# The opening of a fused mixer and feed-forward kernel: first transfers on one queue, in other cuts, and warming products in another order

## The chip, the cores and the metric

The kernel runs on one core of a Trainium2 chip. The metric is the device time of one execution in microseconds; the figure for a kernel is the median over its runs. A profile of one execution gives, for every instruction, its engine, start and length, and for every DMA its issue and landing.

## The reference

One layer of a transformer-like block, batch 1, 256 tokens, width 1024, all in float32. A vector `c` gives six modulation rows (two shifts, two scales, two gates); the block has a mixer and a convolutional feed-forward, each with a modulated input, a gated residual and a layer norm.

```python
mod = silu(c) @ w_ada + b_ada
sh1, sc1, g1, sh2, sc2, g2 = split(mod, 6)
h = x * (1 + sc1) + sh1
y = token_mixer(h, w_in, w_proj_moba, w_proj_ret, w_out)   # proj = h @ w_in, attention + retention
x = layer_norm(ALPHA * x + g1 * y, ln1_g, ln1_b)
h = x * (1 + sc2) + sh2
y = conv_ffn(h, w_ff_gate, w_ff_up, ff_conv_w, ff_conv_b, w_ff_down)
x = layer_norm(ALPHA * x + g2 * y, ln2_g, ln2_b)
```

The change lies wholly in the first microseconds: the first part of `silu(c) @ w_ada`, on which the first tile of `h`, and with it the first product of `h @ w_in`, depends.

## The kernel before

Every weight is streamed once from HBM. A float32 product is made from three: a weight tile `raw` is split by ScalarE into a rounded part `whi` (line 284) and by VectorE into the remainder `wlo` (line 287), the activations likewise into `hh` and `hl`, and TensorE adds `hh*whi`, `hh*wlo` and `hl*whi` (line 301 in the first stage). The order of all work is written out by hand; the queues are in order.

The first stage goes over the eight 128-row slices j of the contraction dimension. For slice j the unit `m{j}` holds the columns of `w_ada` (transposed) that give scale and shift of these 128 channels, 128 x 2048 numbers, 1 MB. VectorE multiplies it with the row `srow` of silu(c), the same in all partitions, and sums along the row; with `bcol` added these are scale and shift (`mod`). Then `h1` makes the tile `hh` from `xT` (line 267 for slice 0), and the tiles `a{j}`, `b{j}`, `g{j}` of `w_in` are split and multiplied.

The list `UNITS` is the order of the loads. `load_A` takes the next one; four buffers `raw` (`RAW_BUFS`) are filled at the start, later ones as buffers come free. `load_cuts` issues one DMA for each pair of column bounds: the first piece on queue `q0`, the others on SP's queue; `then` is called behind the first piece. For `a0b0` that is `load_x(0)`, the load of `xT` for slice 0 (`AYa` in the profile). For `m0`, `q0` is ACT's queue; all other loads go on SP's.

Before all units SP issues `first`, a table of 128 x 56 numbers: `c` in columns (`cT`) and biases. The opening is then:

- ScalarE loads its activation table (line 131), VectorE sets 512 columns of `srow` to zero (line 190), and TensorE multiplies these zeros with each other (line 192, widths `WARM`, results unused).
- With `first` there, line 196 and 197 make silu(c) in columns, and eight transposes (line 204, in `rows`) spread it into two PSUM banks as the row, 512 columns each.
- TensorE makes two products of columns of m0 that nobody reads (line 213, `BUSY`).
- `ada0` (lines 233 to 242) makes scale and shift of slice 0 by four reductions over 512 columns of m0 each (line 238), the first two with the first bank, and adds up (line 242). m0's columns lie in the order scale and shift of the first 512 channels, then of the other 512. ScalarE copies the banks to `srow` (line 206) for the later slices.
- Line 267 makes `hh` of slice 0 in two parts of 128 tokens, `halve("a0", 512)` splits `a0`, and line 301 begins.

Behind the first stage come further projections, attention and retention, the output projection, layer norm, feed-forward and the last norm, all fed by the same stream on SP's queue.

## Time and profile before

| | us |
|---|---|
| median of 3 runs | 423.86 |
| lowest, highest | 423.75, 424.02 |
| profiled execution, its own time | 423.81 |
| its span, first to last instruction | 422.1 |
| TensorE busy in the span | 412.2 |
| VectorE busy | 369.8 |
| ScalarE busy | 245.6 |

Rows of the profile read: line of the kernel, engine, operation, tile written <- tiles read, shape, then count, busy time and length. PE is TensorE, PEld its weight loads, DVE VectorE, ACT ScalarE, POOL GpSimd, SP the engine that issues most DMAs; a q behind a name is its queue. q1 is SP's DMA queue, q10 ACT's. Rows of the timeline begin with start and length, and in brackets stand idle time before and what ended it; consecutive instructions of one kind are merged (x4), with the length of the group. A product of two float32 operands shows as two passes. Matmul lengths are modelled ends; starts are the better measure.

### The profile page before, as it was taken

The page shows a single profiled execution, that of the slowest core. Times are in us where ns is not written, and L with a number is a line of the kernel's source. Part 1 is how long each engine was busy: PE and PEld are TensorE (multiplying, and loading weights), DVE is VectorE, ACT ScalarE, POOL GpSimd, SP SyncE. Part 2 cuts the span into 40 slices and gives each one's busy share as a digit, 9 for nine tenths or more (in the row PEclk, how much of TensorE's full clock was granted, in tenths as well). Part 3 has the DMA queues.
Part 4 walks back from the last instruction along what each step waited for, and adds up shares of the span by engine and source line. Part 5 has one row for each costly group of instructions (what it writes and reads, how often), then busy time and mean ns, then how long its engine had stood idle before and what let it go on. Part 6 is the DMA issues. An engine that isn't in the chain of part 4 may idle for free.

```text
span 422.1 us, 5794 instructions
## 1 busy us (share of the span) xinstructions
PE 412.2 (98%) x2104; PEld 347.9 (82%) x2104; DVE 369.8 (88%) x613; ACT 245.6 (58%) x397; POOL 14.0 (3%) x26
## 2 busy tenths in 40 slices
PE   7999999999999999999999999999999999999993
PEld 4888888888888888888888898888888888888883
DVE  5979899978999999899787887999999888789976
ACT  4666568687876387534554886555555445455700
POOL 0000000100000000001000001000000010012200
PEclk9999999999999999999999999999999999999998
DMA  8997997786479778788672094975865776550002
GB/s 309 405 410 304 419 415 286 242 319 226 186 264 352 280 254 332 313 301 327 233 283 99 2 346 183 374 293 194 302 267 214 278 285 231 187 187 2 1 25 75
DMA packets 18540, 105.58 MB, mean 250 GB/s; under 512 B 2256, under 2 KB 3536, under 8 KB 7760
## 3 DMA queue, kind: packets, MB, share of 16 engines
q1 hardware_dynamic: 16992, 99.70, 62.4%
q0 software_dynamic: 1376, 4.99, 3.2%
q10 hardware_dynamic: 144, 0.52, 0.4%
q8 instruction: 16, 0.26, 0.2%
q14 instruction: 12, 0.10, 0.1%
HBM read 104.15 MB, written 1.06 MB: 249 GB/s over the span
## 4 chain that ended last, share of the span: by engine, by line
PE 96%; DVE 2%; DMA 1%; issue 0%; DVEq 0%; ACT 0%
PE P L115 17%; PE P L116 17%; PE P L117 17%; PE P L124 16%; PE P L301 13%; PE P L126 8%; PE P L688 1%; PE P L691 1%; PE P L690 1%; PE P L993 1%; DMA first<-in_first 1%; PE P L1048 1%; PE P L1071 1%; PE P L1095 1%; DVE unread L238 1%; PE P L1156 0%
## 5 line engine op out<-in xcount | busy, mean ns | idle before, releaser
L1277 DVE TENSOR_TENSOR wlo<-raw,whi 128x1024 fp32r<-128x1024 f32 x118 | 141.7, 1219 | 13.5 <-ACT whi L1263 13.4
L1263 ACT ACTIVATE whi<-raw 128x1024 fp32r<-128x1024 f32 x118 | 122.1, 1056 | 40.8 <-DMA raw<-in_wpr 10.0
L115 PE MATMUL P<-whi,AH 128*128 128x512 f32 x160 | 63.3, 396 | 0.0
L117 PE MATMUL P<-whi,AH 128*128 128x512 f32 x160 | 62.3, 390 | 0.0
L116 PE MATMUL P<-wlo,AH 128*128 128x512 f32 x160 | 62.3, 389 | 0.0
L301 PE MATMUL P<-whi,AH 128*128 128x512 f32 x160 | 41.6, 390 | 0.8 <-DVE AH L267 0.8
L124 PE MATMUL P<-AYa,whi 128*128 128x512 f32 x144 | 39.2, 393 | 0.0
L227 DVE CUSTOM_DVE_ANT_0 junk<-raw,srow 128x1024 bf16<-128x1024 f32 x32 | 39.0, 1219 | 0.0
L124 PE MATMUL P<-AYb,whi 128*128 128x512 f32 x144 | 38.6, 390 | 0.0
L301 PEld LDWEIGHTS P<-whi,AH 128*128 128x128 f32 x160 | 30.0, 188 | 7.8 <-ACT whi L284 1.6
L115 PEld LDWEIGHTS P<-whi,AH 128*128 128x128 f32 x160 | 30.0, 188 | 6.6 <-issue 0.7
L117 PEld LDWEIGHTS P<-whi,AH 128*128 128x128 f32 x160 | 30.0, 188 | 6.4
L116 PEld LDWEIGHTS P<-wlo,AH 128*128 128x128 f32 x160 | 30.1, 188 | 5.9
L465 ACT ACTIVATE A<-P 128x256 f32<-128x256 f32 x36 | 13.7, 381 | 34.4 <-PE P L126 32.5
L124 PEld LDWEIGHTS P<-AYb,whi 128*128 128x128 f32 x144 | 27.0, 188 | 6.0
L284 ACT ACTIVATE whi<-raw 128x512 fp32r<-128x512 f32 (+1 forms) x26 | 20.6, 822 | 16.9 <-DMA raw<-in_strm 15.4
L287 DVE TENSOR_TENSOR wlo<-raw,whi 128x512 fp32r<-128x512 f32 (+1 forms) x26 | 23.3, 935 | 5.5 <-ACT whi L284 5.5
L124 PEld LDWEIGHTS P<-AYa,whi 128*128 128x128 f32 x144 | 25.1, 190 | 3.6
L126 PEld LDWEIGHTS P<-AYa,wlo 128*128 128x128 f32 x144 | 22.0, 189 | 2.8
L301 PE MATMUL P<-wlo,AH 128*128 128x512 f32 x80 | 23.2, 390 | 0.0
L126 PE MATMUL P<-AYb,wlo 128*128 128x256 f32 x144 | 23.1, 283 | 0.0
L126 PE MATMUL P<-AYa,wlo 128*128 128x256 f32 x144 | 22.9, 282 | 0.0
(302 smaller groups left out, 733.2 us busy)
## 6 DMA issues: line engine op xcount, KB each, us to landing
raw<-in_ada SPq DMA_DIRECT2D x16, 1024.0 KB, 5.0
raw<-in_wup SPq DMA_DIRECT2D x11, 1024.0 KB, 4.9
raw<-in_wgate SPq DMA_DIRECT2D x11, 1024.0 KB, 5.1
raw<-in_wdown SPq DMA_DIRECT2D x11, 1024.0 KB, 5.0
raw<-in_winB SPq DMA_DIRECT2D x10, 1024.0 KB, 7.7
raw<-in_strm SPq DMA_DIRECT2D x8, 1024.0 KB, 7.7
raw<-in_strm SPq DMA_DIRECT2D x13, 512.0 KB, 6.9
raw<-in_winGr SPq DMA_DIRECT2D x4, 1024.0 KB, 6.2
```

The source lines that it names most:

```text
L115: pe.matmul(o, lh, rh, start=start, stop=False)
L116: pe.matmul(o, lh, rl, start=False, stop=False)
L117: pe.matmul(o, ll, rh, start=False, stop=stop)
L124: pe.matmul(o, wh[:, k * 128:(k + 1) * 128], x2[k], start=k == 0, stop=False)
L126: pe.matmul(o[:, :256], wl[:, k * 128:(k + 1) * 128], x2[k][:, 0], start=False, stop=k == n - 1)
L227: dve.tensor_tensor_reduce(out=nobody(j if own else None), in0=raw, in1=srow, scale=1.0, scalar=0.0, op0=OP.mult, op1=OP.add, accum_out=mo ...
L284: act.activation(hi[:, o], raw[:, o], AF.Copy)
L287: dve.tensor_tensor(lo[:, o], raw[:, o], f(hi[:, o]), OP.subtract)
L301: pe.matmul(pa[b0 + c // 512 * 2 + t], x[xi][:, j, t * 128:(t + 1) * 128], ws[k][:, c:c + 512], start=first and (xi, k) == (0, 0), stop=la ...
L465: act.activation(t, p[:, 256:], AF.Copy)
L1263: act.activation(hi, src, AF.Copy)
L1277: dve.tensor_tensor(lo, src, f(hi), OP.subtract)
```

## The change

- m0's first piece is issued by SP instead of ACT, so behind `first` on the same queue, and m0 comes in three pieces of 512, 512 and 1024 columns instead of two of 1024.
- `a0b0` comes in two pieces of 1024 columns (a0, then b0) instead of four of 512; `xT` of slice 0 stays behind the first piece.
- The zeroed columns of `srow` are set in two steps, 128 and 384 columns, and the unused products are of 128 and 448 columns instead of 512 and 160. (The loop pairs three banks with two widths, so there are two products, as before.)

```diff
-WARM = (512, 160)
+WARM = (128, 448)
...
-        cuts = Q4 if u == "a0b0" else HALVES if j < 4 and u[0] in "mb" else (0, 2048)
+        cuts = (0, 512, 1024, 2048) if u == "m0" else (0, 1024, 2048) if u == "a0b0" else HALVES if j < 4 and u[0] in "mb" else (0, 2048)
...
-        load_cuts(t, src, cuts, (lambda: load_x(0)) if u == "a0b0" else None, act if u == "m0" else sp)
+        load_cuts(t, src, cuts, (lambda: load_x(0)) if u == "a0b0" else None, sp if u == "m0" else sp)
...
-    dve.memset(srow[:, :512], 0.0)
-    for b, w in zip((4, 5), WARM):
+    for c in (0, 128), (128, 512):
+        dve.memset(srow[:, c[0]:c[1]], 0.0)
+    for b, w in zip((4, 5, 4), WARM):
         pe.matmul(bank(b)[:, :w], srow[:, :128], srow[:, :w], start=True, stop=True)
```

## The prediction

> **What bounds the kernel now.** I read the page's first parts, then the chain that ended last, then the opening in order of time.

> ```profile
> span 422.1 us, 5794 instructions
> PE 412.2 (98%) x2104; PEld 347.9 (82%) x2104; DVE 369.8 (88%) x613; ACT 245.6 (58%) x397; POOL 14.0 (3%) x26
> PE 96%; DVE 2%; DMA 1%; issue 0%; DVEq 0%; ACT 0%
> 0.81 3.12 DMA first<-in_first
> 4.50 1.10 PE P L204 x4
> 5.62 0.40 DVE unread L238
> 6.93 0.60 DVE unread L238
> 8.39 0.36 DVE AH L267
> 8.88 54.72 PE P L301 x240
> 415.02 0.43 DVE A7b L578
> ```

> The last rows are pieces of the chain (start, length, what). From 8.88 to 415 us it is TensorE without a gap that matters; before it stands a serial opening: small table, four transposes, VectorE's reductions over m0, the first stationary tile. So the change can win what L301 starts sooner, if the feed afterwards keeps up. The profiled execution took 423.81 us (its span and 1.7 us around it), 0.05 below the 423.86 median; I subtract from the median.

> The opening in order of time (start, length, engine and line; x counts merged instructions):

> ```profile
> 0.80 0.40 ACTq L102 DMA_DIRECT2D raw<-in_strm  x1
> 0.81 0.37 SPq L136 DMA_DIRECT2D first<-in_first  x1
> 0.88 0.06 DVE L141 MEMSET epst<- 128x1 f32 x1 [0.88 <-PEq L1423]
> 1.01 0.48 DVE L190 MEMSET srow<- 128x512 f32 x1
> 1.23 0.89 SPq L102 DMA_DIRECT2D raw<-in_strm  x2
> 1.24 1.28 ACT L131 ACT_TABLE_LOAD   x1 [1.24 <-PEq L1423]
> 1.55 2.61 PE L192 MATMUL P<-srow 128*128 128x512 f32 x4 [1.55 <-DVE srow L190]
> 2.57 1.06 PE L192 MATMUL P<-srow 128*128 128x512 f32 x1
> 3.42 0.34 PEld L192 LDWEIGHTS P<-srow 128*128 128x128 f32 x1 [0.52 <-issue]
> 3.69 0.47 PE L192 MATMUL P<-srow 128*128 128x160 f32 x1
> 5.17 0.54 PE L204 MATMUL P<-ident,sc 128*128 128x128 f32 x2
> 5.54 0.49 PE L204 MATMUL P<-ident,sc 128*128 128x128 f32 x3
> 5.87 2.21 PE L213 MATMUL P<-raw 128*128 128x512 f32 x4
> 7.53 1.14 ACT L284 ACTIVATE whi<-raw 128x512 fp32r<-128x512 f32 x2
> 8.39 0.60 DVE L267 TENSOR_SCALAR AH<-AYa,mod 128x128 fp32r<-128x128 f32 x2
> ```

> **The change, step by step.** *Warming products.* The one-column memset takes 0.06, that of 512 columns 0.48, so about 0.06 plus 0.42/512 per column: 128 columns end at 1.01 + 0.165 = 1.18, and TensorE, which began 0.06 after the memset, begins at 1.24 instead of 1.55. The other 384 columns (0.38) end before the first product does. Each product is two passes; the second 512-column pass runs from 2.57 to 3.42, 1.66 ns a column, and the very first took 0.17 more. The loop pairs three banks with two widths, so two products remain, 128 + 448 = 576 columns: 576 x 2 x 1.66 ns = 1.91, and the engine is free at 1.24 + 0.17 + 1.91 = 3.32 us. Before it was free at 3.69 + 0.27 = 3.96 and then waited for the transposes' input until 4.50.

> *The small table.* It now has the DMA engines alone at first; before, the first half of m0 (512 KB) started on ACT's queue 0.01 us earlier. What that did, in packets (count, MB, share) by queue, q1 being SP's and q10 ACT's, for 1.8 to 1.9 us and for 3.4 to 3.5 us:

> ```profile
> q10 hardware_dynamic: 4, 0.02, 87.2%
> q1 hardware_dynamic: 41, 0.01, 41.1%
> q10 hardware_dynamic: 12, 0.05, 131.4%
> q1 hardware_dynamic: 1, 0.00, 0.6%
> ```

> 41 small packets went in the first tenth of a microsecond, and one was still going at 3.4 us, between 4 KB packets of m0. The table's landing at 3.93 (0.81 + 3.12) is 0.4 us behind its last packets. Alone, its packets should be through by about 2.2 and it lands near 2.6: that is my value; the other end is 3.93, no change. From landing to transposes it was 0.57 (3.93 to 4.50), so anything up to 2.75 is hidden under the warming products. ACT is no obstacle: without its DMA issue (0.40) its 1.28 us table load starts about 0.84 and the small activation behind it (0.20) ends near 2.35. So the transposes begin at 3.32, and the first reduction 1.12 later (4.50 to 5.62 before): 4.44, a gain of 1.18 at this point. It does not reach the end of the opening, as the loads show.

> *m0 and what is behind it.* SP issues as many DMAs up to g0 as before (first, three for m0, two for a0b0, x0, g0; before first, one, four, x0, g0), ACT's issue goes. m0's first piece is issued at 1.23 instead of 0.80.

> ```profile
> raw<-in_strm SPq DMA_DIRECT2D x1, 512.0 KB, 4.7
> raw<-in_strm SPq DMA_DIRECT2D x1, 256.0 KB, 5.0
> AYa<-in_strm SPq DMA_DIRECT2D x1, 128.0 KB, 4.9
> 2.17 0.43 SPq L163 DMA_DIRECT2D AYa<-in_strm  x1
> GB/s 0 41 224 353 418 369 399 389 416 414 410 400 407 406 414 410 410 389 406 418 393 422 386 405 410 438 438 385 410 426 377 408 432 410 373 74 16 106 319 426
> ```

> The last line is GB/s in each microsecond from 0 to 40: from 4 to 34 us the DMA engines are full, so landings go by bytes, not by issue. Second half of m0: issue 1.23, landing 5.93. Next quarter of a0b0: 1.70 + 5.0 = 6.70; x0: 2.17 + 4.9 = 7.07. Now x0 stands behind 1024 columns of a0 instead of 512: 512 KB (0.524 MB) at the 414 GB/s that large packets reach is 1.27, x0 itself 0.37 (6.70 to 7.07): 5.93 + 1.27 + 0.37 = 7.57, plus a delay d of the stream in front of it. One part is known: half of m0 now goes in 2 KB packets, which a0b0's rows from 5 to 8 us show at 386 GB/s (mean of 369, 399, 389): 0.09 more than at 414. The other is the later start: at most the 0.43 by which the issue moves; below, the stream no longer shares its first microsecond with small packets (224 GB/s from 2 to 3 us against 400 later), which from 2.25 on could put it 0.16 ahead. So d lies between -0.07 and 0.52; no row is nearer to one end, and I take the middle, 0.22: x0 at 7.79.

> [...]

> *VectorE's opening.* m0's cuts of 512 columns are wanted at 4.44 and 5.05 and land, counted back from 5.93 + d at 395 GB/s, at 4.16 and 4.82. The last is wanted 1.31 after the first reduction (5.62 to 6.93), at 5.75, and lands at 6.15: VectorE waits 0.4. From that third reduction to L267 it is 1.46 (6.93 to 8.39): 6.15 + 0.04 + 1.46 = 7.65. L267 also reads x0, which ends last: 7.79 + 0.04 = 7.83. L301 follows 0.49 later (8.88 - 8.39): **8.32 us, 0.56 sooner**. By the same count the table may land as late as 3.3 at no cost. ACT needs whi of a0: a0's half lands at 5.93 + 1.27 + 0.22 = 7.42, two activations end at 7.42 + 1.14 = 8.56, the first near 8.0, and the second is read by the third product, half a microsecond after the start: hidden, by 0.3.

> *Will the feed keep up?* TensorE moves 0.56 earlier; the stream, d later behind m0, gets back 0.18 when a0b0 goes in large packets, so it is 0.04 late. The tightest rows, tile a1 and, for comparison, tile b3's stationary part:

> ```profile
> 20.75 0.33 SPq L102 DMA_DIRECT2D raw<-in_a1a  x1
> 26.26 2.43 PE L301 MATMUL P<-whi,AH 128*128 128x512 f32 x10
> 26.45 0.60 ACT L269 ACTIVATE AH<-AYb,mod 128x256 fp32r<-128x256 f32 x1 [0.24 <-DVE mod L260]
> 30.60 1.06 ACT L284 ACTIVATE whi<-raw 128x1024 fp32r<-128x1024 f32 x1 [1.49 <-DMA raw<-in_a1a]
> 31.69 1.23 DVE L287 TENSOR_TENSOR wlo<-raw,whi 128x1024 fp32r<-128x1024 f32 x1 [1.85 <-ACT whi L284]
> 33.74 0.39 PE L301 MATMUL P<-wlo,AH 128*128 128x512 f32 x1
> ```

> a1's low part is ready at 31.69 + 1.23 = 32.92 and read at 33.74: 0.82 of slack, of which 0.56 + 0.04 is used. b3's stationary tile is ready at 27.05 and read eight products into the group of ten, 28.08: 1.03. So 0.22 is left and no stall comes; after 34 us the stream idles (74, 16 GB/s), loads wait for buffers and move with TensorE. Sum: 423.86 - 0.56 = **423.30 us**.

> **Rivals.** (A) *The stream is the new bound.* With d = 0.52, x0 lands at 8.09, L267 starts at 8.13 and gains 0.26: 423.60. For it: every load to 34 us is DMA-paced, ACT waits 1.49 for a1; against it: the shared first microsecond.
> (B) *The table lands as late alone as beside m0.* Then the transposes stay at 4.50 and nothing moves: 423.86. Against it stand the 41 packets in the first 0.1 us.
> (C) *Slower: TensorE's clock falls back.* L192 ran 0.85 us per 512-column pass, while the four passes of L213 took 2.21 with a stall in them, and L301 began 0.80 after they ended (5.87 + 2.21 = 8.08) at full pace. If the warm state is missed or lost before L301, as many microseconds as it took to warm up run at half pace (1.55 to about 5.4, where the transposes' starts close up: two from 5.17, 0.2 apart, then three within 0.22 from 5.54): 1.9 lost, 423.30 + 1.9 = 425.2. For it: 96 columns fewer are warmed with, and the gap grows. Transposes at 3.32, eight at 0.21 to 5.0, L213 2.21 to 7.2, so 1.1 of idleness before 8.32. Against it: work begins 0.31 sooner and has no hole (0.54 before, 3.96 to 4.50), so 3.85 us of it are over at 5.1, and 0.80 of idleness cost nothing. It decides if 1.1 does. [...]
> (D) *More than forecast.* The stream starts at full rate, d = -0.07 or less: x0 at 7.50, L267 at 7.54, VectorE's own chain (5.86 + 0.04 + 1.46 = 7.36) is no bound: gain 0.85 or more, 422.95.

> **How the numbers follow.** Chances: forecast 0.54, A 0.20, B 0.06, C 0.09, D 0.11. A measurement of this kernel tells about 0.2%, 0.85 us, from no change; forecast, A and B lie within it: 0.80; D beyond it, 0.11; C slower, 0.09. The forecast's own range is 423.1 to 423.5; with A, B and half of D, 422.9 to 424.0, which leaves out C and the other edge of D.

> **What would show it.** TensorE's first product at about 1.24; the table landing before 3.3 (2.6 expected); L204 at 3.32; first L238 at 4.44 and the third after a wait for m0's last cut, at 6.2; L267 at 7.83, waiting for x0 and not for `mod`; L301 at 8.32 with passes at full pace; no wait of TensorE at a1 near 33. Wrong if L204 still waits for the table, if L267 stands at 8.1 or later behind x0, if L301's first passes take 0.43 apart, or if a gap of TensorE between 17 and 34 us gives the start back.

## The result: slower by 4.9 us, and the profile after

| | before | after |
|---|---|---|
| median, us | 423.93 (4 runs) | 428.81 (4 runs) |
| lowest, highest | 423.75, 424.02 | 428.08, 429.12 |
| profiled execution | 423.81 | 429.12 |
| its span | 422.1 | 427.4 |

The ratio is 1.0114, 95% interval 1.0102 to 1.0126. The forecast was 423.30 with a range of 422.9 to 424.0: wrong in sign and far outside the range. When the changed kernel was run again later it gave 425.01 to 428.99 (median 427.83), while the kernel before stayed within 0.6 us beside it; single executions of the changed kernel therefore differ by more than most effects below.

The opening after, from the timeline, in order of time (start, length; the bracket gives idle time before and what ended it). Lines from 190 on are one higher than before.

```profile
1.15 2.29 PE L193 MATMUL P<-srow 128*128 128x128 f32 x4 [1.15 <-DVE srow L191]
2.48 0.21 ACT L197 ACTIVATE sc<-first 128x8 f32<-128x8 f32 x1 [0.18 <-DMA first<-in_first]
3.24 1.92 PE L205 MATMUL P<-ident,sc 128*128 128x128 f32 x8
4.39 0.69 DVE L239 CUSTOM_DVE_ANT_0 unread<-P,raw 128x512 bf16<-128x512 f32 x1 [1.22 <-PE P L205]
4.94 3.10 PE L214 MATMUL P<-raw 128*128 128x512 f32 x4
5.53 0.69 DVE L239 CUSTOM_DVE_ANT_0 unread<-P,raw 128x512 bf16<-128x512 f32 x1 [0.44 <-DMA raw<-in_strm]
9.43 0.69 DVE L239 CUSTOM_DVE_ANT_0 unread<-P,raw 128x512 bf16<-128x512 f32 x1 [3.20 <-DMA raw<-in_strm]
10.62 1.15 ACT L285 ACTIVATE whi<-raw 128x512 fp32r<-128x512 f32 x2 [3.69 <-DMA raw<-in_strm]
11.04 0.60 DVE L268 TENSOR_SCALAR AH<-AYa,mod 128x128 fp32r<-128x128 f32 x2
11.54 2.04 PE L302 MATMUL P<-whi,AH 128*128 128x512 f32 x4 [3.49 <-DVE AH L268]
```

Down to the first reduction (4.39) everything came within 0.15 us of the forecast. Then VectorE waits 3.20 us for m0's third cut, which lands at 9.29 (issued 2.18, 7.1 on its way) instead of 6.15, and all behind it is late with it. Instead of 0.56 sooner, the first stage starts 2.66 later than before (11.54 against 8.88).

The first stage's row in the chain that ended last, after:

```profile
11.54 57.28 PE P L302 x240
```

Its transfers: the issues of m0's third cut and of x0 with KB and us to landing, and GB/s in each microsecond from 0 to 40:

```profile
raw<-in_strm SPq DMA_DIRECT2D x1, 512.0 KB, 7.1
AYa<-in_strm SPq DMA_DIRECT2D x1, 128.0 KB, 7.8
GB/s 0 22 146 305 236 328 328 281 367 397 389 414 421 399 409 410 377 397 388 308 401 381 389 414 392 419 430 434 410 434 393 426 385 393 344 417 361 139 8 0
```

From 4 to 8 us the stream moves 236, 328, 328, 281 GB/s where before it moved 418, 369, 399, 389: 0.40 MB less. The DMA engines are busy for most of that time. These are packets, MB and share of SP's queue from 4 to 5 us, first after:

```profile
q1 hardware_dynamic: 90, 0.24, 90.9%
```

and before:

```profile
q1 hardware_dynamic: 105, 0.41, 102.2%
```

A packet takes 16 engines x 0.909 us / 90 = 0.162 us for 2.7 KB, against 0.156 for 3.9 KB before (0.41 MB / 105): half as long again for each KB. That is a mean, and the trace's packet records from 4 to 8 us show what is behind it. The median packet of 4096 bytes took 0.159 us in both kernels. But 15 of the 414 packets after took over 0.4 us, up to 2.41 us (one that began at 5.39), and hold a fifth of the packet time; before, it was 1 of 804. All packets together took 59.4 us, against 65.7 before. So a few packets are stretched to many times their length, and the engines are busy for about a tenth less.

The second half of the loss stands in the length of that merged row: 57.28 us for the same 240 products that took 54.72. By stretches of 2 us (busy time of TensorE, its weight loads, VectorE, ScalarE, POOL, then the granted clock, DMA share, GB/s), after:

```profile
8.00:10.00 2.00, 0.04 (x1) 0.00 (x0) 0.57 (x1) 0.00 (x0) 0.00 (x0) 1.00 1.00 382
10.00:12.00 2.00, 0.47 (x1) 0.50 (x2) 1.85 (x8) 1.38 (x3) 0.00 (x0) 0.56 1.01 401
12.00:14.00 2.00, 2.00 (x6) 1.52 (x6) 1.91 (x5) 2.00 (x5) 0.00 (x0) 0.50 1.03 410
14.00:16.00 2.00, 2.00 (x7) 1.51 (x6) 1.83 (x3) 0.98 (x2) 0.00 (x0) 0.50 1.04 409
16.00:18.00 2.00, 2.00 (x8) 1.63 (x7) 2.00 (x3) 2.00 (x5) 0.00 (x0) 0.73 1.01 387
```

In these rows the clock is full until 10.24 us (0.56 x 2 = 0.24 + 1.76/2), then half until 17.07 (0.73 x 2 = 0.93 + 1.07/2), two stretches of 3.41 us. While it is half, the products start 0.43 us apart (12.10, 12.52, 12.95) instead of 0.23. Late load 2.66 and slow passes 57.28 - 54.72 = 2.56 make 5.2 of the 5.3 us between the spans.

### The profile page after: what moved, and what is told of

Same layout as the page of the kernel before. It is cut to its first block, busy times and chain, and to the rows that moved or that the text cites. A ratio compares the mean times of both kernels' runs of the same rounds, so it can differ in the third digit from the quotient of the medians.

```text
span 427.4 us, 5792 instructions
## 1 busy us (share of the span) xinstructions
PE 415.5 (97%) x2104; PEld 350.3 (82%) x2104; DVE 370.2 (87%) x614; ACT 245.9 (58%) x397; POOL 14.0 (3%) x26
## 3 DMA queue, kind: packets, MB, share of 16 engines
HBM read 104.15 MB, written 1.06 MB: 246 GB/s over the span
## 4 chain that ended last, share of the span: by engine, by line
PE 96%; DMA 2%; DVE 1%; SPq 0%; issue 0%; DVEq 0%
PE P L115 17%; PE P L117 17%; PE P L116 17%; PE P L124 15%; PE P L302 13%; PE P L126 8%; DMA AYa<-in_strm 2%; PE P L692 1%; PE P L689 1%; PE P L691 1%; PE P L994 1%; PE P L1049 1%; PE P L1072 1%; PE P L1096 1%; PE P L1157 0%; PE P L633 0%
## 5 line engine op out<-in xcount | busy, mean ns | idle before, releaser
L115 PE MATMUL P<-whi,AH 128*128 128x512 f32 x160 | 63.3, 396 | 0.0
L117 PE MATMUL P<-whi,AH 128*128 128x512 f32 x160 | 62.3, 390 | 0.0
L302 PE MATMUL P<-whi,AH 128*128 128x512 f32 x160 | 43.4, 403 | 3.5 <-DVE AH L268 3.5
L302 PEld LDWEIGHTS P<-whi,AH 128*128 128x128 f32 x160 | 31.3, 196 | 10.9 <-ACT whi L285 4.3
L115 PEld LDWEIGHTS P<-whi,AH 128*128 128x128 f32 x160 | 30.1, 188 | 6.6 <-issue 0.7
L117 PEld LDWEIGHTS P<-whi,AH 128*128 128x128 f32 x160 | 30.0, 188 | 6.3
## 6 DMA issues: line engine op xcount, KB each, us to landing
raw<-in_strm SPq DMA_DIRECT2D x15, 512.0 KB, 7.8
```

What stands on the lines that cost most here:

```text
L115: pe.matmul(o, lh, rh, start=start, stop=False)
L117: pe.matmul(o, ll, rh, start=False, stop=stop)
L302: pe.matmul(pa[b0 + c // 512 * 2 + t], x[xi][:, j, t * 128:(t + 1) * 128], ws[k][:, c:c + 512], start=first and (xi, k) == (0, 0), stop=la ...
```

## The experiments

All ratios are against runs of the kernel before on the same chip (medians 423.82 to 423.97). "Start" is the first product of the first stage, 8.88 in the profile before. Landings are of one profiled execution.

### Each part alone

**Only the warming products** (before, with the new memset and widths):

```diff
-WARM = (512, 160)
+WARM = (128, 448)
-    dve.memset(srow[:, :512], 0.0)
-    for b, w in zip((4, 5), WARM):
+    for c in (0, 128), (128, 512):
+        dve.memset(srow[:, c[0]:c[1]], 0.0)
+    for b, w in zip((4, 5, 4), WARM):
```

> The kernel before with the new warming products alone (128 and 448 columns, zeros set in two steps); loads as before. Both theories on the loads expect no change of them: small table at 3.9 us, m0's second half at 5.9, L301 at about 8.9, 423.9 us within 0.3. If the new warming alone lets TensorE's clock turn later (in the changed kernel it turned near 6.7 us instead of 5.4), the two unread products of m0's columns would still run at half pace here and L301 would begin at full or half pace depending on it: at most 2.6 us more.

424.24 us, ratio 1.0014 [1.0004, 1.0024]. The table still landed beside m0 (4.07), the start was 9.02 and the clock was still half at 6.38: the first unread pass took 0.85 us there, against 0.43 in the kernel before. TensorE's products end sooner, in front of a table that is as late as before, and so leave a larger hole (1.20 us of idleness instead of 0.34); that this hole delays the clock is likely, but no run isolates it. The cost is about 0.4 us.

**Only the queue** (before, m0's first half issued by SP):

```diff
-        load_cuts(t, src, cuts, ..., act if u == "m0" else sp)
+        load_cuts(t, src, cuts, ..., sp)
```

> The kernel before with one edit: m0's first half is issued by SP, behind the small table, still in two pieces of 1024 columns; a0b0 in four pieces as before. Theory Q (one queue instead of two is what makes packets stall in the first microseconds): m0's second half lands near 9 us instead of 5.9, L301 starts 2 us late or more and at half pace, 427 to 429 us. Theory P (the 512-column pieces do it): m0 lands within 0.5 of 5.9, the table at 2.5, 423.5 to 424.2.

423.76 us, ratio 1.0000 [0.9990, 1.0009]; table 2.44, m0 at 5.17 and 6.46, x0 at 7.52, start 8.63. The issue on SP is not the loss. Its stream, and the start:

```profile
GB/s 0 21 115 287 422 388 392 373 399 401 434 406 390 417 406 414 406 398 396 410 422 406 401 392 407 410 467 393 410 410 434 369 420 408 426 205 41 164 311 434
```

And in order of time:

```profile
8.63 1.15 PE L301 MATMUL P<-whi,AH 128*128 128x512 f32 x4 [0.91 <-DVE AH L267]
```

**Only a0b0 in two pieces** (before, Q4 replaced):

```diff
-        cuts = Q4 if u == "a0b0" else ...
+        cuts = (0, 1024, 2048) if u == "a0b0" else ...
```

> The kernel before with one edit: a0b0 in two pieces of 1024 columns, xT of slice 0 behind the first of them. Theory Q: m0's halves land as before (4.7 and 5.9), only xT comes 0.65 later, at 7.7, still ahead of the 8.39 at which it is read: 423.9 within 0.3. Theory P': the larger pieces behind m0 hold it up: m0's second half lands later than 7 and the time rises by 1 us or more.

424.41 us, ratio 1.0013 [1.0003, 1.0022]; m0 at 4.77 and 6.06, x0 at 7.74, start 8.96. A small loss.

**More of the unread products** (the changed kernel, to keep the clock):

```diff
-BUSY = 2
+BUSY = 5
```

> The changed kernel with five unread products of m0's columns instead of two, so that TensorE works until about 10.4 us. Theory K (half of the loss is the clock: TensorE idles for 3.5 us before L301, which then runs at half pace until 17 us and ends 2.56 late): L301 starts at 11.5 as in the changed kernel but at 0.23 a product from the first, 426.2 us. Rival: the clock is not lost to the idle time but was never steady; then L301 still begins at half pace and the time stays at 428.8.

427.15 us, ratio 1.0079 [1.0064, 1.0094]. The clock stayed full (first four products in 1.17), m0 landed at 8.96 and the start was 11.19, 2.31 late: the late load alone. The span is 3.5 longer than before. Of the 1.2 more, 1.1 lies in the first stage, whose 240 products took 55.82 us; the chain that ended last runs there over loads issued at 14.27, 24.23, 40.11 and 51.46 and comes to the stage's products only at 61.28, for the last 24. The next load was issued at 14.27 instead of 10.82, and the stream fell into a hole that the changed kernel does not have there (the 144, 25 and 123 from 13 to 16 us). That this hole causes the 1.1 is not shown. The start, and then the stream:

```profile
11.19 1.17 PE L302 MATMUL P<-whi,AH 128*128 128x512 f32 x4 [0.52 <-DVE AH L268]
```

Its transfers, GB/s by microsecond:

```profile
GB/s 0 21 166 330 279 299 316 335 393 401 426 418 396 144 25 123 340 426 422 414 401 422 401 410 418 410 383 412 414 434 401 410 434 418 381 397 426 410 205 66
```

### Which loads

**m0's cuts of 512, 512, 1024 on SP, all else as before:**

```diff
-        cuts = Q4 if u == "a0b0" else ...
+        cuts = (0, 512, 1024, 2048) if u == "m0" else Q4 if u == "a0b0" else ...
-        load_cuts(t, src, cuts, ..., act if u == "m0" else sp)
+        load_cuts(t, src, cuts, ..., sp)
```

> The kernel before with m0 wholly on SP's queue in 512, 512 and 1024 columns; a0b0 still in four pieces, warming as before. Theory P (the 512-column pieces at the head of the one queue make the packets behind them stall): m0's last cut lands at 8 us or later, L301 starts at 10.5 or later, 426 to 429 us. Theory R (the one queue together with a0b0's two large pieces does it): m0's last cut lands near 6.1, L301 at 8.3 to 8.8, 423.4 to 424.0.

425.77 us (424.34 to 427.26), ratio 1.0046 [1.0028, 1.0064]; m0 at 4.12, 5.12 and 8.60. Against the run with only the queue changed, this adds the cuts alone: 2.0 us, and the stall is there (the profiled execution, 426.97, is one of the slower ones). Its transfers, GB/s by microsecond:

```profile
GB/s 0 19 145 365 221 252 259 245 334 406 406 418 422 409 406 407 406 422 397 401 406 397 422 406 400 399 400 442 422 401 426 418 393 390 418 405 295 115 0 0
```

And in order of time:

```profile
8.73 0.69 DVE L238 CUSTOM_DVE_ANT_0 unread<-P,raw 128x512 bf16<-128x512 f32 x1 [2.37 <-DMA raw<-in_strm]
10.77 2.05 PE L301 MATMUL P<-whi,AH 128*128 128x512 f32 x4 [2.24 <-DVE AH L267]
```

**The same cuts, first piece on ACT's queue as before:**

```diff
-        cuts = Q4 if u == "a0b0" else ...
+        cuts = (0, 512, 1024, 2048) if u == "m0" else Q4 if u == "a0b0" else ...
```

> The kernel before with m0 in 512, 512 and 1024 columns, the first piece on ACT's queue as before, the others on SP's; a0b0 in four pieces. Theory P in its wide form (small pieces of m0 in whatever queue): late as in the run above, over 426. In its narrow form (only on one queue) and theory R: table at about 3.7, L301 at 8.7 to 9.0, 423.6 to 424.2.

424.47 us, ratio 1.0011 [1.0002, 1.0021]; table 3.45, m0 3.74, 4.40, 6.89, start 9.06. Most of the stall is gone with one 512-column piece on the other queue: from 4 to 8 us the stream moves 354, 261, 352, 376 GB/s. The profiled execution (423.88) is the fastest of ten, and the median lies above the 423.6 to 424.2 expected.

**Queue and a0b0's pieces, m0 in halves:**

```diff
-        cuts = Q4 if u == "a0b0" else ...
+        cuts = (0, 1024, 2048) if u == "a0b0" else ...
-        ... act if u == "m0" else sp)
+        ... sp)
```

> The kernel before with m0 on SP's queue in two halves and a0b0 in two halves; warming as before. Theory R: m0's second half lands at 8 us or later, 426 to 429. Theory P: it lands near 6.0, xT near 7.8, L301 at 8.6 to 9.0, 423.6 to 424.4.

424.12 us, ratio 1.0009 [0.9999, 1.0018]; m0 5.07 and 6.34, x0 8.55, start 9.14: no stall in m0.

**All of the changed loads, with the old warming products:**

```diff
-WARM = (128, 448)
+WARM = (512, 160)
-    for c in (0, 128), (128, 512):
-        dve.memset(srow[:, c[0]:c[1]], 0.0)
-    for b, w in zip((4, 5, 4), WARM):
+    dve.memset(srow[:, :512], 0.0)
+    for b, w in zip((4, 5), WARM):
```

> The changed kernel with the old warming (512 and 160 columns): all edits of the loads together, none of the warming. Theories P and R: the loads are late as in the changed kernel (m0's last cut at 9 us, L301 at about 11.5, at half pace), 428 to 429. Theory W (TensorE's earlier start has a part in it): m0 lands by 6.5 and the time is below 425.

427.40 us (424.66 to 429.39), ratio 1.0084 [1.0059, 1.0108]. The loads do it without the new warming. The median is 1.6 us above that of the cuts on SP alone, so a0b0's large pieces may add to the stall, though alone they cost 0.5; the two intervals overlap. The profiled execution was the mildest of seven (424.66): m0 at 7.01, start 9.66 after 2.18 us of idleness, at full pace:

```profile
9.66 1.17 PE L301 MATMUL P<-whi,AH 128*128 128x512 f32 x4 [2.18 <-DVE AH L267]
```

### Size and place of the pieces

**The changed kernel again, and the changed kernel with m0 in two halves**, together on one chip:

```diff
-        cuts = (0, 512, 1024, 2048) if u == "m0" else ...
+        cuts = (0, 1024, 2048) if u == "m0" else ...
```

> The changed kernel once more, for its spread beside the others of this call. If the late loads are its own and not of one chip or one moment: m0's last cut lands after 7 us, L301 starts after 10 us, median 427 to 429.5, single runs up to 2.5 us apart as in the kernel with all edits of the loads alone (424.7 to 429.4).

> The changed kernel with one thing undone: m0 in two halves of 1024 columns, on SP's queue; a0b0 in halves and the new warming as in the changed kernel. Theory P (m0's 512-column pieces cause the late loads): m0's second half lands at 6.0 to 6.6, xT by 8.6, L301 at 8.6 to 9.3, 423.8 to 424.9, so 4 us of the loss are gone. Theory S (it takes all the edits together, or the early start of TensorE): m0 lands after 7.5 and the time stays over 427.

427.83 (ratio 1.0087 [1.0056, 1.0118]) against 424.04 (1.0004 [0.9995, 1.0013]). This is the deciding pair: one pair of column bounds is worth 3.8 us. With halves, GB/s by microsecond and the second half's issue:

```profile
GB/s 0 22 158 291 418 401 400 435 397 430 410 399 396 400 414 418 401 393 406 401 422 406 408 388 405 434 422 410 426 410 397 397 398 416 456 90 16 188 377 401
raw<-in_strm SPq DMA_DIRECT2D x1, 512.0 KB, 4.8
```

And in order of time:

```profile
5.33 0.69 DVE L239 CUSTOM_DVE_ANT_0 unread<-P,raw 128x512 bf16<-128x512 f32 x1 [2.00 <-DMA raw<-in_strm]
8.24 0.60 DVE L268 TENSOR_SCALAR AH<-AYa,mod 128x128 fp32r<-128x128 f32 x2
8.73 1.16 PE L302 MATMUL P<-whi,AH 128*128 128x512 f32 x4 [1.12 <-DVE AH L268]
```

The stream moves about 400 GB/s from 4 us on, m0's second half (issued 1.70) lands at 6.49, and TensorE idles 1.12 us and keeps its clock (first four products in 1.16). It starts 0.15 sooner than before, and the time shows nothing of that.

**m0 in four pieces of 512:**

```diff
-        cuts = Q4 if u == "a0b0" else ...
+        cuts = Q4 if u in ("m0", "a0b0") else ...
-        ... act if u == "m0" else sp)
+        ... sp)
```

> The kernel before with m0 on SP's queue in four pieces of 512 columns (a0b0 in four too, old warming). Theory M (the change from 2 KB to 4 KB packets in the first microseconds makes them stall, as the first long packets are those of m0's third cut): no stall, m0's last cut at 6.3 to 6.8, 423.6 to 424.4. Theory P (small pieces at the head are enough): m0's last cut after 7.5, over 425.

424.96 us, ratio 1.0025 [1.0015, 1.0035]; cuts at 4.03, 4.70, 6.49, 7.19, start 8.81. A milder dip (338, 297, 340 GB/s from 4 to 7 us), between what the two theories expected: more small pieces were not worse than two. The start is not late here; the first stage's 240 products took 55.68 us instead of 54.72, and 0.36 of that lies in the first four (1.51 instead of 1.15).

**m0 as 1024, 512, 512:**

```diff
-        cuts = Q4 if u == "a0b0" else ...
+        cuts = (0, 1024, 1536, 2048) if u == "m0" else Q4 if u == "a0b0" else ...
-        ... act if u == "m0" else sp)
+        ... sp)
```

> The kernel before with m0 on SP's queue in 1024, 512 and 512 columns (a0b0 in four, old warming). Theories M and P both: large packets first, as in the run with the queue alone, so m0's last cut lands at 6.3 to 6.8, L301 at 8.5 to 8.9, 423.5 to 424.2. If it is late all the same (after 7.5, over 425), then it is three transfers to m0 and not the size of the first that counts.

424.05 us, ratio 1.0005 [0.9996, 1.0015], start 8.60. The same two small pieces behind the large one cost no time that can be measured. But they are not free of the dip: the rate from 4 to 8 us is 373, 346, 376, 362, and m0's last cut landed at 7.01, later than the 6.3 to 6.8 expected and than the 6.46 with the queue alone.

### The clock alone, and what else stalls

**Thirteen small products behind the unread ones** (changed kernel):

```diff
+    for i in range(13):
+        pe.matmul(bank(5)[:, :128], ident, ident, start=True, stop=True)
```

> The changed kernel with 13 more unread products, of the 128 x 128 identity with itself, behind the two of m0's columns: TensorE works on until about 11 us without holding a load buffer. If half pace from L301 on is the whole second part of the loss: L301 at about 11.4 with 0.23 a product from the first, and the median falls by up to 2.5 us, to 425.5 to 426.5, with a spread of the late loads alone. If the clock falls back although TensorE works: no change, 427.8 to 428.8.

429.30 us, ratio 1.0127 [1.0112, 1.0143]. Mis-sized: 26 passes took 7.04 us, 0.27 each, and ended at 14.8, long after the stationary tile was there (VectorE began it at 10.15). The start was 14.53, so a full clock was bought with almost 4 us of filler. One thing it does show: with a full clock the first stage took 54.68 us, and the span is 5.7 longer for a start 5.65 later. So without the slow passes the later start is the whole loss.

**Five of them:**

```diff
+    for i in range(5):
+        pe.matmul(bank(5)[:, :128], ident, ident, start=True, stop=True)
```

> The changed kernel with 5 products of the identity behind the two of m0's columns, so that TensorE works until about 10.4 us and L301 waits for nothing but its data. With 13 of them L301 began at 14.53 at full pace and the span was 5.7 us over that of the kernel before, for 5.65 of later start; so at full pace the loss is the later start alone. If that holds: L301 at 10.7 to 11.5, 0.23 a product from the first, span 1.9 to 2.6 over the one before, median near 426. If half pace comes back: 428 or more.

427.68 us (425.22 to 428.41), ratio 1.0070 [1.0042, 1.0099]. The filler ended at 9.55, 1.78 us before the first product, and the clock fell all the same, from 11.08 to 14.49 (0.77 x 2 = 1.08 + 0.92/2; 0.88 x 2 = 1.52 + 0.48/2). In order of time:

```profile
6.88 2.67 PE L216 MATMUL P<-ident 128*128 128x128 f32 x10
11.33 2.05 PE L304 MATMUL P<-whi,AH 128*128 128x512 f32 x4 [1.78 <-DVE AH L270]
```

And by stretches of 2 us:

```profile
10.00:12.00 2.00, 0.67 (x2) 0.60 (x3) 1.87 (x7) 1.58 (x4) 0.00 (x0) 0.77 1.01 410
12.00:14.00 2.00, 2.00 (x6) 1.56 (x5) 1.91 (x5) 2.00 (x5) 0.00 (x0) 0.50 1.03 409
14.00:16.00 2.00, 2.00 (x9) 1.60 (x8) 1.82 (x3) 1.38 (x3) 0.00 (x0) 0.88 1.03 410
```

**a0b0 in four pieces of 512 and x0 ahead of m0** (cuts of m0 as in the change, all on SP):

```diff
-UNITS = ("m0", "a0b0", "g0", ...
+UNITS = ("a0b0", "m0", "g0", ...
```

> m0 on SP's queue in 512, 512 and 1024 columns, but a0b0 (four pieces) and xT ahead of it; old warming. The order of the loads makes L301 late by the 2.8 us that a0b0 takes; what is asked is the rate. If small pieces stall only as the first of the program: over 380 GB/s in every microsecond from 5 on and no stretched packets among m0's cuts, about 426 to 427 us. If the same cuts of m0 stall wherever they stand: under 320 GB/s for 3 us behind them, 428 or more.

429.11 us, ratio 1.0122 [1.0107, 1.0137]; start 14.03, 5.15 late where 2.8 had been expected. The time itself is that of a longer way to m0; what counts is the stream: now a0b0's own small pieces stall, at 209 and 191 GB/s from 4 to 6 us, and m0's cuts behind them land 0.7 and 1.3 us apart. So it is not m0's data that is slow.

```profile
GB/s 0 22 117 332 209 191 340 379 356 377 418 393 422 330 64 131 332 418 336 360 328 333 335 389 385 418 415 394 424 422 426 442 393 401 410 385 412 449 400 157
```

**The same with a0b0 in two pieces:**

```diff
-        cuts = Q4 if u == "a0b0" else ...
+        cuts = (0, 1024, 2048) if u == "a0b0" else ...
```

> a0b0 in two pieces of 1024 columns and xT ahead of m0, then m0 in 512, 512 and 1024 columns, all on SP's queue; old warming. If small pieces stall only as the first of the program: over 370 GB/s in every microsecond from 4 on, m0's last cut near 9.0, L301 at 11 to 12. If m0's small cuts stall wherever they stand: under 320 GB/s for 3 us behind them, m0's last cut after 10.5.

428.54 us, ratio 1.0106 [1.0088, 1.0124]; start 13.21. From 4 to 8 us 342, 373, 318, 324: neither the full stream nor the deep stall that the two theories expected. That small pieces stall only at the very head is not shown by this run.

**m0's third cut on ACT's queue, the two small ones on SP's** (before, otherwise):

```diff
-            (sp if c0 else q0).dma_start(t[:, c0:c1], src[:, c0:c1])
+            if q0 is act and c0 == 1024:
+                late.append((t[:, c0:c1], src[:, c0:c1]))
+                continue
+            (sp if c0 or q0 is act else q0).dma_start(t[:, c0:c1], src[:, c0:c1])
...
-        cuts = Q4 if u == "a0b0" else ...
+        cuts = (0, 512, 1024, 2048) if u == "m0" else Q4 if u == "a0b0" else ...
...
     table(AF.Sigmoid)
+    act.dma_start(*late.pop())
```

> m0 in 512, 512 and 1024 columns, the first two on SP's queue behind the table, the third on ACT's queue behind its table load (issued near 2.3); a0b0 in four, old warming. If the stall needs a single queue: m0's third cut lands by 6.5, L301 at 8.3 to 8.8, 423.4 to 424.0, the best of all. If small pieces at the head stall on any queue: third cut after 7, 424.5 or more.

423.78 us, ratio 0.9995 [0.9985, 1.0004]. The third cut was issued at 0.98, ahead of the time expected (2.3) and of the small cuts (1.25), and landed first, at 4.87; the small ones at 5.54 and 6.21; table 2.63; start 8.94. The stream:

```profile
GB/s 0 22 232 322 385 387 397 375 313 381 397 422 406 414 418 410 401 409 396 408 410 401 422 390 405 406 438 430 401 401 426 377 408 440 414 180 41 115 303 426
```

Both small pieces are there, and no stall: 385, 387, 397, 375 from 4 to 8 us. As the large cut came first here as well, the run does not tell if the second queue or the order did it. No version was measurably faster than the kernel before; this one and the queue alone equal it.

## Why the prediction was wrong, step by step

| step | forecast | after | with m0 in halves |
|---|---|---|---|
| first warming product | 1.24 | 1.15 | 1.15 |
| table lands | 2.6 | 2.45 | 2.61 |
| transposes | 3.32 | 3.24 | 3.23 |
| first reduction | 4.44 | 4.39 | 5.33 |
| m0's last landing | 6.15 | 9.29 | 6.49 |
| a0's half lands | 7.42 | 10.60 | 7.79 |
| x0 lands | 7.79 | 10.94 | 8.14 |
| first stationary tile | 7.83 | 11.04 | 8.24 |
| first product | 8.32 | 11.54 | 8.73 |

*Warming products and small table: right.* The table alone landed at 2.45, so rival B fell: beside 512 KB on the other queue it had taken until 3.93, and no wait of TensorE for it was left. Also right is that this gain (5.62 to 4.39, 1.23 us at the first reduction, 1.18 forecast) does not reach the first product: m0 and x0 decide.

*m0 and what is behind it: the step that failed.* It is the term d, taken as 0.22 between -0.07 and 0.52. Measured against its own baseline, 5.93 (5.98 in the trace's records), it is 9.29 - 5.93 = 3.36. Two parts of its working fell:

- The price of 2 KB packets. It was read from a0b0's rows from 5 to 8 us, 386 GB/s, and carried to the first microseconds: 0.09 us. There the same size of piece, in front of a 1024-column one on a single queue, brought the stream down to 236 to 328 GB/s. So the bounds of d rested on a price that had been seen only with the stream already full: the size of the piece was the same, its place in the program was not.
- The lower bound. It held that m0 alone in its first microsecond goes faster than beside the small packets. The halves show that it does not. In the packet records m0's first packet starts at 1.88 before and at 2.26 with halves, and from there both move the same: 0.35 MB of large packets in 1.5 us, 0.54 MB in 2.0 us. So the later issue is paid in full, as in rival A: d is 6.49 - 5.93 = 0.56, above the upper bound for the delay alone (0.43), and x0 landed at 8.14 (8.09 in rival A). Even without the stall the gain at the first product would have been 0.15 (8.73) instead of 0.56.

*VectorE's chain, x0, L267 to the first product:* right in form. x0 lands 1.65 after m0 in after as in the halves (10.94 - 9.29, 8.14 - 6.49), forecast 7.79 - 6.15 = 1.64. The stationary tile comes 0.10 behind x0 (forecast 0.04) and the product 0.50 behind that (0.49). The chain carried the delay through unaltered. One term in it was too small, without effect: from the third reduction to the stationary tile it is 1.61 (after) and 1.62 (halves), not 1.46, so VectorE was ready with `mod` no more than 0.02 before x0.

*The feed afterwards:* no stall of TensorE at a1 near 33 us; with the start 2.66 later the question did not arise, and in the halves TensorE lost nothing there either (54.68 us for the 240 products). Where the start came sooner with other cuts, part of it was given back: 55.24 us with 1024, 512, 512 and 55.68 with four pieces.

*Rival C, the clock:* named with 0.09, and it happened, but as a consequence of the late load and not of the changed warming (with the cuts alone and the old warming it fell too). It was to decide if 1.1 us of idleness is too much. With the halves that case was run: 1.12 us of idleness cost nothing. With 3.49 the clock fell, and cost 2.56 instead of 1.9, since it stayed half for two stretches of 3.41 us where I had taken one warming time. In after the last 2.20 us before the fall at 10.24 were idle (the last pass ended at 8.04), in the run with five small products the last 1.53 before the fall at 11.08 (the filler ended at 9.55).

*Accounting.* Excess of the start over 8.88, and of the span over 422.1, in the profiled executions:

| kernel | start later | span longer | clock |
|---|---|---|---|
| after | 2.66 | 5.3 | half from 10.24 to 17.07 |
| after, again | 2.51 | 5.2 | half at the start (11.39), to about 17 |
| cuts on SP alone | 1.89 | 3.2 | half from 10.40 to 13.82 |
| five small products | 2.45 | 4.0 | half from 11.08 to 14.49 |
| five unread products | 2.31 | 3.5 | full; 1.1 more in the first stage |
| thirteen small products | 5.65 | 5.7 | full |
| changed loads, old warming | 0.78 | 0.8 | full |

In the three runs of the table with a full clock the span grew by the later start and by what the first stage took longer, within about 0.1 us. So in the changed kernel about half of the loss is the late load, and half the clock that falls in the wait for it.

*What is shown and what is open.* Shown: the cuts of 512 columns cause the late load (two pairs: 427.83 to 424.04, and 423.76 to 425.77), with them a few packets take many times as long (up to 2.41 us beside a median of 0.159), and the queue, a0b0's pieces and the warming products cost 0.6 us or less each when made alone. Shown as well: it is not m0's data, and the time is that of the kernel before with the large cut first, on the same queue or on the other one. Not shown: why these packets stretch; if it is the 2 KB rows or the number and size of the pieces, which always changed together; and if a second queue helps without a change of order. That a small piece must be first fits the changed kernel, the reordered one and the one with the large piece first, but behind large pieces, of a0b0 or of m0, there was still a milder dip. The depth differs from run to run of one kernel (425.01 to 428.99), so one profile for each kernel ranks the mild cases only roughly.

## What to carry to other kernels

The price read in the middle of the saturated stream (386 GB/s for pieces of 512 columns) did not hold for this program's first transfers (236 to 328 GB/s). If a small piece at the head of a queue is to make data come sooner, look in the trace at when the pieces behind it land, and try the same cut with a large piece in front, on the same queue or on a second one. A late load on the path to the first product had a second price here: TensorE's clock fell in the wait of 3.49 us that it left, which cost 2.56 us beside the 2.66 of the later start. When an edit bundles cuts, queues and order, run each of them alone and the bundle without each.
